# The split of cross head 0's read-back probabilities, moved ahead of head 2's scores

## The chip, the cores and the metric

The kernel runs on one core of a Trainium2 chip. Five engines work from queues of their own: TensorE (PE in the profile; PEld are its weight loads), VectorE (DVE), ScalarE (ACT), GpSimd (POOL) and SyncE (SP), which only issues transfers. The metric is the time of one execution on the device, in microseconds (us). Before the change it is 383.32 us, the median of three runs (382.92 to 384.19).

## What is computed

One decoder layer for 256 tokens of width 1024: a mixer (causal pooling and self-attention in 8 heads), a cross-attention in 4 heads into 256 memory tokens, and a gated feed-forward of width 2816, each followed by a layer norm. The change lies in the cross-attention:

```python
def memory_cross_attention(h, mem, w_xq, w_xkv, w_xo):
    B_, S_, D = h.shape
    M = mem.shape[1]
    q = (h @ w_xq).reshape(B_, S_, XATTN_HEADS, XATTN_HEAD_DIM)
    kv = mem @ w_xkv
    k = kv[..., :D].reshape(B_, M, XATTN_HEADS, XATTN_HEAD_DIM)
    v = kv[..., D:].reshape(B_, M, XATTN_HEADS, XATTN_HEAD_DIM)
    s = jnp.einsum('bshd,bmhd->bhsm', q, k,
                   preferred_element_type=jnp.float32) * (XATTN_HEAD_DIM ** -0.5)
    p = jax.nn.softmax(s, axis=-1)
    o = jnp.einsum('bhsm,bmhd->bshd', p.astype(v.dtype), v).reshape(B_, S_, D)
    return o @ w_xo
```

All of it is float32. The kernel gets there with rounded products: each operand is split into a rounded high half and a low half (what the rounding left), and a product is high x high, high x low and low x high.

## The kernel before

**Splits.** `split` (L318) makes the two halves of a tile: ACT casts it to the high half (L319), DVE subtracts that from the tile to get the low half (L320). The queries are split and scaled in the same way by `split_scaled` (L323 on ACT, L324 on DVE). Weights come in by `Stream`: SP loads a raw tile, ACT casts it (L99), DVE subtracts (L100); tiles are called w0 to w124 in the order of use, with h, l and r for high, low and raw. `three` (L256 to L258) issues the three products of a pair of split operands.

**The cross-attention, head by head** (heads 0 to 3). `do_xq(h)` is a generator of the query projection: 8 steps of 6 products each, for the weights w43 to w50; `run(xq[h], n)` takes n steps. `xscores(h)` makes the scores (12 products into the bank `xs`), the row maximum on DVE (`mx`, L440), the exponentials on ACT (L429), and the scaling on DVE (L434, L436). The probabilities must then be transposed for the product with the values. For heads 0 to 2 this goes through memory: `xprobs_out(h)` turns 32 x 32 blocks on DVE (L340) into a staging tile, also named `xs`, and POOL's queue writes it to memory (`xd<-xs`, L343); `xprobs_in(h)` reads it back in four quarters on the same queue (`xr<-xd`, L351); `xprobs_split(h)` splits what was read back into the pair `xst`. Head 3 is transposed on TensorE instead (`xprobs_pe`, L762). `xattend(h)` multiplies `xst` with the values (12 products into `xo`) and splits the result into `oT`. `project(c_xo, ...)` is the output projection (512-wide products into `acc`), whose steps are run between the heads.

**The staging tiles.** The tiles `xs` (staged), `xr` (read back) and `xst` (split) come from one pool with the tag "pair" and three buffers. A new tile takes a place that is free, and its first writer waits until the last user of that place is done. So where a tile is asked for, in the order of the code, decides whose end it waits for. Before the change the places go round as follows (A, B and C are the three buffers, from the built programs):

| buffer | before | after |
| --- | --- | --- |
| A | xs of head 0, xr of head 1, xst of head 2 | the same |
| B | xr of head 0, xst of head 1, xst of head 3 | xr of head 0, xs of head 2, xr of head 2 |
| C | xs of head 1, xs of head 2, xst of head 0, xr of head 2 | xs of head 1, xst of head 0, xst of head 1, xst of head 3 |

**What sets the order.** The order of each engine's instructions is that of the code (a manual schedule): every call above appends to the engines' queues, and an engine works through its own. The calls around the change are at L775 to L808.

Of the kernel before, what the change touches and what calls it, by code (L numbers as in the profile page):

```python
# [125 lines left out]
def decoder_layer(  # L126
# [183 lines left out]
    def run(gen, n=None):  # L310

        while n is None or n > 0:
            if next(gen, gen) is gen:
                return False
            n = None if n is None else n - 1
        return True

    def split(h, l, ps):  # L318
        nc.scalar.copy(h, ps)  # L319
        nc.vector.tensor_sub(l, ps, r32(h))  # L320
# [408 lines left out]
    def do_xq(h):  # L729
        ps = (bank if h == 0 else accbank)("pxq").rearrange("p (f t) -> p f t", f=2)  # L730
        yield from proj_t([ps[:, f, :] for f in range(2)], c_xq[h], h1T)
        xqT[h] = [sp.tile([P, 2, S], F32R, name=f"xq{i}", tag="pr", bufs=PR_BUFS) for i in range(2)]
        split_scaled(*xqT[h], ps, 256 ** -0.5)

    def xscores(h):
        ps = bank("xs").rearrange("p (t s) -> p t s", t=2)
        for t in range(T):
            for kk in range(2):
                three(ps[:, t, :], pair(xqT[h], ALL, kk, slice(t * P, (t + 1) * P)), pair(xkT, ALL, 2 * h + kk),
                      kk == 0, kk == 1)  # L740
        pr = sp.tile([P, 2, T, P], F32, name="xpr", tag="pr", bufs=PR_BUFS)
        by_t = pr.rearrange("p s t b -> p t s b")
        scaled(by_t, exps(by_t, ps.rearrange("p t (s b) -> p t s b", s=2), negmax(ps)))
        xpr[h] = pr

    def xprobs_out(h):
        turnsx[h] = turned([(0, xpr[h].rearrange("p s t b -> p (s t) b"))], 4, "x", nc.gpsimd)

    def xprobs_in(h):
        turnsx[h] = landed(turnsx[h], 4, "x", queue=nc.gpsimd)  # L750

    def xprobs_split(h):
        raw = turnsx[h].rearrange("p i m b -> p m i b")
        st = sp.tile([P, 2, 2, S], F32R, name="xst", tag="pair", bufs=3)
        xpt[h] = st[:, 0], st[:, 1]
        split(*[x.rearrange("p s (t i b) -> p (s t) i b", t=T, i=4) for x in xpt[h]], raw)
# [18 lines left out]
    xq = [do_xq(h) for h in range(XH)]  # L775
# [10 lines left out]
    run(xq[2])  # L786
    run(xq[3], 3)
    xprobs_in(1)
    run(xq[3], 2)
    xscores(2)  # L790
    xprobs_out(2)
    xprobs_split(0)
    run(xq[3])

    h2 = ap.tile([P, T, D], F32, tag="a8", name="h2")
# [178 lines left out]
```

## Time and profile before

| | us |
| --- | --- |
| median of three runs | 383.32 |
| the profiled execution | 383.19 |
| its span, from its first to its last instruction | 381.4 |
| TensorE busy | 369.1 (97%) |
| VectorE busy | 262.4 (69%) |
| ScalarE busy | 177.6 (47%) |
| GpSimd busy | 34.6 (9%) |

Times inside the profile count from the start of its span. A row of the timeline has the start, the duration, the engine, the line, the operation, what is written `<-` what is read, the shape, and in brackets how long the engine sat idle before it and what ended that. Matmuls overlap, so their pace is read from the distance of their starts, not from their durations. In the list of waits the numbers are the total in us, the count and the longest.

The cross-attention and the start of its output projection lie between about 125 and 180 us. TensorE goes from one product to the next through the whole span, with the exceptions that the prediction shows. In the view of stretches a row has the length, then the busy time of PE, PEld, DVE, ACT and POOL, then TensorE's mean granted clock as a share of full speed, the DMA engines' busy share, and GB/s.

### The profile page before, as it was taken

Reading aid. Unit: us, or ns where it says so; the run is one execution under the profiler, and the core shown is the slowest. Engines: PE = TensorE matmul, PEld = TensorE weight load, DVE = VectorE, ACT = ScalarE, POOL = GpSimd, SP = SyncE. Lnnn points to the kernel's source line nnn. Section 1 sums busy time; section 2 is a strip of 40 time slices with the busy share of each in tenths; the row PEclk is TensorE's granted clock in tenths of the full one; section 3 lists DMA queues with packets and bytes.
Section 4 is the critical chain, followed back from the end, with each engine's and each line's share of the span. In section 5 each row is a group of like instructions: output and inputs, shape, how many; then the busy total and the mean of one; then the engine's idle time right before and its main releaser. Section 6 shows DMA issues by size and latency. Waiting matters only on the chain.

```text
span 381.4 us, 5523 instructions
## 1 busy us (share of the span) xinstructions
PE 369.1 (97%) x2024; PEld 319.0 (84%) x2024; DVE 262.4 (69%) x388; ACT 177.6 (47%) x259; POOL 34.6 (9%) x66
## 2 busy tenths in 40 slices
PE   9999999999999999699999999999999999999992
PEld 9997998997878999588878888888888888888881
DVE  4768898974798976455789866666666666454275
ACT  5756775653153854244229454454545454444000
POOL 1000157140110004120100000000000000000000
PEclk9999999999999999889999999999999999999997
DMA  7997699799337976555106988888789987730011
GB/s 243 411 413 283 232 318 280 257 259 365 115 137 240 384 274 222 159 184 168 56 2 209 380 290 264 232 251 250 236 232 290 296 263 241 211 107 0 0 48 63
DMA packets 32540, 84.52 MB, mean 222 GB/s; under 512 B 4097, under 2 KB 12161, under 8 KB 32385
## 3 DMA queue, kind: packets, MB, share of 16 engines
q1 hardware_dynamic: 30224, 79.05, 63.1%
q0 software_dynamic: 1712, 4.72, 4.0%
q10 hardware_dynamic: 576, 0.39, 0.3%
q8 instruction: 16, 0.26, 0.3%
q14 instruction: 12, 0.09, 0.1%
HBM read 76.81 MB, written 7.34 MB: 221 GB/s over the span
## 4 chain that ended last, share of the span: by engine, by line
PE 81%; issue 11%; DVE 2%; DMA 2%; POOL 2%; ACT 0%; DVEq 0%; POOLq 0%; ACTq 0%
PE pg L258 10%; PE pg L257 10%; PE pg L256 10%; PE acc L256 9%; PE acc L257 9%; PE acc L258 9%; PE pxk L274 6%; PE pqk L392 6%; PE pu L274 3%; DMA xd<-xs 2%; PE busy L363 1%; PE pv L256 1%; POOL xr L351 1%; PE pv L257 1%; PE pv L258 1%
## 5 line engine op out<-in xcount | busy, mean ns | idle before, releaser
L623 POOL TENSOR_TENSOR rs<-rs,mhalf 128x1 f32<-128x1 f32 x6 | 5.4, 898 | 235.4 <-DVE rs L622 235.4
L834 ACT ACTIVATE sg<-pg 128x256 f32<-128x256 f32 x22 | 8.4, 384 | 12.9 <-PE pg L258 12.8
L612 DVE SCALAR_TENSOR_TENSOR r<-h,acc 128x256 f32<-128x256 f32 (+1 forms) x10 | 5.1, 520 | 10.9 <-PE acc L258 10.9
L835 DVE TENSOR_TENSOR sg<-sg,pg 128x256 f32<-128x256 f32 x22 | 9.2, 420 | 4.0 <-ACT sg L834 2.6
L429 ACT ACTIVATE pr<-pr,mx 128x128 f32<-128x128 f32 (+1 forms) x16 | 7.1, 445 | 8.7 <-DVE mx L460 8.7
L351 POOL DMA_DIRECT2D pt<-pd x16 | 8.8, 555 | 7.3 <-DMA pd<-ps 4.5
L320 DVE TENSOR_TENSOR gTl<-gr,gTh 128x512 fp32r<-128x512 f32 x11 | 7.6, 687 | 1.8 <-ACT gTh L319 1.8
L319 ACT CAST gTh<-gr 128x512 fp32r<-128x512 f32 x11 | 6.8, 617 | 4.0 <-DMA gr<-gd 4.0
L319 ACT CAST h2Th<-tp 128x512 fp32r<-128x512 f32 x4 | 2.3, 587 | 13.5 <-PE tp L330 13.4
L615 DVE BATCH_NORM_STATS2 st<-r 128x6 f32<-128x512 f32 (+1 forms) x14 | 8.1, 580 | 0.5
L256 PE MATMUL xo<-xst,xv 128*128 128x256 f32 x16 | 5.2, 326 | 3.3 <-ACT xst L319 3.3
L429 ACT ACTIVATE xpr<-xs,mx 128x256 f32<-128x256 f32 x8 | 3.7, 470 | 9.4 <-DVE mx L440 9.4
L628 DVE SCALAR_TENSOR_TENSOR r<-r,mv,g 128x512 f32<-128x512 f32 x11 | 7.8, 743 | 0.0
L340 DVE STREAM_TRANSPOSE gs<-sg 128x512 f32<-128x512 f32 x11 | 7.7, 704 | 0.0
L351 POOL DMA_DIRECT2D xr<-xd x12 | 6.5, 550 | 12.2 <-PE xo L258 6.8
L343 POOL DMA_DIRECT2D pd<-ps x4 | 2.5, 612 | 51.1 <-DVE ps L340 50.8
L256 PEld LDWEIGHTS xo<-xst,xv 128*128 128x128 f32 x16 | 3.6, 224 | 3.6 <-ACT xst L319 3.5
L320 DVE TENSOR_TENSOR oTl<-xo,oTh 128x512 fp32r<-128x512 f32 x4 | 2.8, 692 | 5.4 <-ACT oTh L319 5.4
L319 ACT CAST oTh<-xo 128x512 fp32r<-128x512 f32 x4 | 2.3, 587 | 7.5 <-PE xo L258 7.5
L434 DVE RECIPROCAL sm<-sm 128x2 f32<-128x2 f32 x12 | 2.0, 165 | 5.5 <-ACT xpr L429 4.4
L436 DVE TENSOR_SCALAR pr<-pr,sm 128x128 f32<-128x128 f32 (+1 forms) x16 | 5.5, 391 | 0.3
L634 DVE SCALAR_TENSOR_TENSOR h<-r,rs,b 128x512 f32<-128x512 f32 x8 | 5.6, 745 | 0.0
(1092 smaller groups left out, 1419.5 us busy)
## 6 DMA issues: line engine op xcount, KB each, us to landing
gd<-gs SPq DMA_DIRECT2D x11, 256.0 KB, 5.1
gr<-gd SPq DMA_DIRECT2D x44, 64.0 KB, 4.7
pd<-ps POOLq DMA_DIRECT2D x4, 384.0 KB, 4.5
pt<-pd POOLq DMA_DIRECT2D x16, 96.0 KB, 7.8
g<-in_ln_g SPq DMA_DIRECT2D x3, 512.0 KB, 7.4
b<-in_ln_b SPq DMA_DIRECT2D x3, 512.0 KB, 7.1
wr<-in_w_qkv SPq DMA_DIRECT2D x5, 256.0 KB, 4.8
mr<-in_mem_t SPq DMA_DIRECT2D x1, 1024.0 KB, 11.2
```

What stands on the lines that cost most here:

```text
L256: nc.tensor.matmul(ps, wa, ya, start=start, stop=False, skip_group_check=part)
L257: nc.tensor.matmul(ps, wa, yb, start=False, stop=False, skip_group_check=part)
L258: nc.tensor.matmul(ps, wb, ya, start=False, stop=stop, skip_group_check=part)
L274: nc.tensor.matmul(pss[f], w[:, s], y, start=k == 0 and f == 0 and n == 0, stop=k == KD - 1 and n == 2, skip_group_check=True)
L319: nc.scalar.copy(h, ps)
L320: nc.vector.tensor_sub(l, ps, r32(h))
L351: queue.dma_start(raw[32 * j:32 * (j + 1)].rearrange("p i m b -> p i (m b)"), via[:, j, :].rearrange("(i a) r -> a i r", i=4))
L392: nc.tensor.matmul(qk[i][:, f, :], w[:, c * P:(c + 1) * P], y, start=k == 0 and f == 0 and w is hi and y is x_hi, stop=k == KD - 1 and w i ...
L429: nc.scalar.activation(dst[:, j, :], src[:, j, :], AF.Exp, bias=mx[:, j:j + 1], scale=sign, accum_out=sm[:, j:j + 1])
L615: nc.vector.bn_stats(self.st[:, self.n, :], self.r[:, c0:c1])
L834: nc.scalar.activation(sg, ps[:, :CW].rearrange("p (f b) -> p f b", f=2), AF.Silu, bias=0.0, scale=1.0)
L835: nc.vector.tensor_mul(sg, sg, ps[:, CW:].rearrange("p (f b) -> p f b", f=2))
```

## The change

`xprobs_split(0)` is called one step of head 3's query projection earlier than head 2's scores, instead of behind `xprobs_out(2)`. Nothing is added, removed or resized.

```diff
     run(xq[3], 3)
     xprobs_in(1)
-    run(xq[3], 2)
+    run(xq[3], 1)
+    xprobs_split(0)
+    run(xq[3], 1)
     xscores(2)
     xprobs_out(2)
-    xprobs_split(0)
     run(xq[3])
```

On ACT the place is behind the cast of w56, where the exponentials of head 2 stood (both names are without buffer numbers; DMASW and a digit is the counter of a transfer on POOL's queue, and the level that is awaited is not shown):

```order
 L99 CAST w56h<-w56r 128x1024 [waits DMAHW7_49]
-L429 ACTIVATE xpr,sm<-xs,mx 128x2x128 [waits DVE_49]
-L429 ACTIVATE xpr,sm<-xs,mx 128x2x128
 L319 CAST xst<-xr 128x512 [waits DMASW5_49,DMASW6_49,DMASW1_49,DMASW7_49,DMASW0_49,DVE_49]
+L429 ACTIVATE xpr,sm<-xs,mx 128x2x128 [waits DVE_49]
+L429 ACTIVATE xpr,sm<-xs,mx 128x2x128
 L99 CAST w57h<-w57r 128x1024 [waits DMAHW0_49,PE_49]
 L323 ACTIVATE xq_1869<-pxq 128x512 [waits PE_49,Activation_49]
```

The cast of head 0's `xst` now stands ahead of head 2's two exponentials. The counters 5, 6, 7 and 0 are those of the four quarters of head 0's read-back, 1 is that of head 1's write-out, and 6 is used again for head 2's write-out: before the change the level awaited on it is one transfer higher.

On DVE the place is behind the subtraction for w56; what follows up to the new queries of head 3 (`xq_1870`) is head 2's softmax and the turning of its blocks:

```order
 L100 TENSOR_TENSOR w56l<-w56r,w56h 128x1024 [waits DMAHW7_49,Activation_49]
+L320 TENSOR_TENSOR xst<-xr,xst 128x512 [waits DMASW5_49,DMASW6_49,DMASW1_49,DMASW7_49,DMASW0_49,Activation_49]
 L440 TENSOR_REDUCE mx<-xs 128x2 [waits PE_49]
 L434 RECIPROCAL sm<-sm 128x2 [waits Activation_49]
 L436 TENSOR_SCALAR xpr<-xpr,sm 128x2x128 [waits DVE_49]
 L436 TENSOR_SCALAR xpr<-xpr,sm 128x2x128
-L340 STREAM_TRANSPOSE xs<-xpr 128x4x4x32 [waits DMASW1_49,DVE_49]
-L320 TENSOR_TENSOR xst<-xr,xst 128x512 [waits DMASW6_49,DMASW5_49,DMASW7_49,DMASW0_49,Activation_49]
+L340 STREAM_TRANSPOSE xs<-xpr 128x4x4x32 [waits DMASW3_49,DVE_49]
 L100 TENSOR_TENSOR w57l<-w57r,w57h 128x1024 [waits DMAHW0_49,PE_49,Activation_49]
 L324 SCALAR_TENSOR_TENSOR xq_1870<-pxq,xq_1869 128x512 [waits Activation_49]
```

The subtraction moved ahead of head 2's maximum, and head 1's write-out (counter 1) is now awaited by the split and no longer by the turning of head 2's blocks, which waits on 3 for a much earlier write-out of the self-attention that used buffer B.

On POOL, behind head 2's write-out, the order of transfers is the same; the read-back of head 2 begins with another wait, since it goes to another buffer:

```order
 L343 DMA xd<-xs 128x512 [waits DMASW6_49,DVE_49]
-L351 DMA xr<-xd 32x4x128 [waits DMAHW1_49,DMAHW2_49,DMASW7_49,DMAHW3_49,DMASW6_49,DMAHW4_49,DVE_49,PE_49]
-L351 DMA xr<-xd 32x4x128 [waits DMASW0_49]
-L351 DMA xr<-xd 32x4x128
+L351 DMA xr<-xd 32x4x128 [waits DMASW6_49,DMASW7_49,DMASW0_49,Activation_49]
+L351 DMA xr<-xd 32x4x128 x2
 L351 DMA xr<-xd 32x4x128 [waits DMASW2_49]
```

It waited for TensorE before (the attention of head 0, whose `xst` held buffer C) and now for the write-out of head 2 and for ACT. On TensorE and SP no instruction moves.

## Prediction

> **What bounds the kernel now.** I read the page's busy times first, then the list of who waited for whom, then the chain that ended last, and only then the matmuls one by one.
>
> ```profile
> PE 369.1 (97%) x2024; PEld 319.0 (84%) x2024; DVE 262.4 (69%) x388; ACT 177.6 (47%) x259; POOL 34.6 (9%) x66
> ...
> PE xo L256 <- ACT xst L319: 3.3, 1, 3.3
> PE busy L363 <- PEq L938: 0.8, 1, 0.8
> PE tp L330 <- DVE h L634: 0.3, 1, 0.3
> PE xv L256 <- DVE r L612: 0.3, 1, 0.3
> ```
>
> The first row says that TensorE (PE) sets the time: 97% of a span of 381.4 us. The others are all the waits of its matmuls. One is large: 3.3 us at the first product of the attention of cross head 0 (`xo`), for ScalarE's half of the split `xst`. The chain of waits says what this cast itself waited for:
>
> ```profile
> 147.82 2.56 DMA xd<-xs
> ...
> 155.02 2.77 DMA xd<-xs
> ...
> 157.97 0.63 ACT xst L319
> 158.62 0.70 DVE xst L320
> ...
> 159.37 0.58 PE xo L257
> ```
>
> The cast started 0.18 us after the write-out `xd<-xs` issued at 155.02 had landed (155.02 + 2.77 = 157.79). That is head 2's write-out, which has nothing to do with head 0's data. It matters because `xst` was put in the place of head 2's staging tile `xs`. Head 0's own data had been read back long before; the rows for the four quarters of head 0, then of head 1, are:
>
> ```profile
> 144.07 2.18 POOL L351 DMA_DIRECT2D xr<-xd  x4 [2.85 <-DMA xd<-xs]
> DMA to landing us min/median/max: 3.6/3.8/4.3
> ...
> 150.91 2.17 POOL L351 DMA_DIRECT2D xr<-xd  x4 [2.53 <-DMA xd<-xs]
> DMA to landing us min/median/max: 4.2/5.0/5.5
> ```
>
> The last quarter of head 0 was issued about 145.7 (144.07 + 3 x 0.55), so it had landed by 145.7 + 4.3 = 150.0 at the latest. The matmuls around the hole, each row's first column being its start:
>
> ```profile
> 149.74 0.28 PE L256 MATMUL xs<-xkTh,xq 128*128 128x256 f32 x1
> ...
> 151.18 0.28 PE L274 MATMUL pxq<-h1Th,w49h 128*128 128x256 f32 x1
> ...
> 155.02 0.28 PE L274 MATMUL pxq<-h1Th,w50l 128*128 128x256 f32 x1
> 158.64 0.58 PE L256 MATMUL xo<-xst,xv 128*128 128x256 f32 x1 [3.34 <-ACT xst L319]
> 159.37 0.58 PE L257 MATMUL xo<-xst,xv 128*128 128x256 f32 x1
> ...
> 161.88 0.41 PE L256 MATMUL xs<-xkTh,xq 128*128 128x256 f32 x1
> ...
> 164.44 0.63 PE L256 MATMUL acc<-w51h,oTh 128*128 128x512 f32 x1
> ...
> 165.55 0.40 PE L256 MATMUL acc<-w51h,oTh 128*128 128x512 f32 x1
> ...
> 167.63 0.28 PE L256 MATMUL xo<-xst,xv 128*128 128x256 f32 x1
> ```
>
> Undisturbed, the 12 products of head 2's scores take 151.18 - 149.74 = 1.44 us, 0.12 us a start; nine 512-wide products take 167.63 - 165.55 = 2.08 us, 0.231 a start. Behind the hole the same 12 scores (161.88 to 164.44) take 2.56 us. The stretches, with the granted clock (third number from the right), say why:
>
> ```profile
> 158.00:159.00 1.00, 0.36 (x1) 0.29 (x1) 0.38 (x1) 1.00 (x2) 0.00 (x0) 0.75 0.00 0
> 160.00:165.00 5.00, 5.00 (x24) 4.90 (x24) 3.00 (x5) 1.13 (x3) 2.17 (x4) 0.50 0.64 211
> 165.00:166.00 1.00, 1.00 (x5) 0.79 (x4) 0.37 (x1) 0.59 (x3) 0.00 (x0) 0.83 0.83 217
> 106.00:108.00 2.00, 1.72 (x9) 1.11 (x7) 1.93 (x4) 1.52 (x2) 0.00 (x0) 1.00 0.60 244
> ```
>
> The clock fell to 0.50 at about 158.5 (0.75 is half a microsecond of it) and came back at about 165.34 (0.83 is a third), so it was low for 6.8 us; after the 0.28 us rest near 107.9 it stayed at 1.00. The hole costs twice: the wait, and the slow matmuls behind it. [...]
>
> **The change part by part.** Nothing is added or removed: one cast on ACT and one subtraction on DVE stand earlier, ahead of head 2's exponentials and maximum. TensorE's own order is the same.
>
> *What goes.* From the last query product (155.02) to head 1's attention (167.63) TensorE takes 12.61 us before. Undisturbed, it is 25 starts of 0.12 (itself, 12 `xo`, 12 `xs`) and 12 of 0.231: 3.00 + 2.77 = 5.77. The surplus is **6.84 us**, made of the wait 158.64 - 155.14 = 3.50; the second product's wait for the subtraction, 0.73 - 0.12 = 0.61; 23 slow starts, (164.44 - 159.37) - 23 x 0.12 = 2.31; and 12 partly slow wide ones, 3.19 - 2.77 = 0.42.
>
> *What is late next.* The split now takes the place of head 1's staging tile, free when head 1's write-out lands at 147.82 + 2.56 = 150.38, later than its data (150.0). I take the reaction of 0.18 us seen above. ACT and DVE then stand thus in the trace of before:
>
> ```profile
> 148.69 1.04 ACT L99 CAST w56h<-w56r 128x1024 fp32r<-128x1024 f32 x1
> 152.11 0.47 ACT L429 ACTIVATE xpr<-xs,mx 128x256 f32<-128x256 f32 x1 [2.37 <-DVE mx L440]
> ...
> 158.50 1.04 ACT L99 CAST w57h<-w57r 128x1024 fp32r<-128x1024 f32 x1
> 159.44 0.59 ACT L323 ACTIVATE xq<-pxq 128x512 fp32r<-128x512 f32 x1
> ...
> 172.96 0.62 ACT L319 CAST xst<-xr 128x512 fp32r<-128x512 f32 x1
> ...
> 146.81 0.71 DVE L340 STREAM_TRANSPOSE xs<-xpr 128x512 f32<-128x512 f32 x1
> 147.45 1.19 DVE L100 TENSOR_TENSOR w55l<-w55r,w55h 128x1024 fp32r<-128x1024 f32 x1
> ...
> 151.38 0.69 DVE L440 TENSOR_REDUCE mx<-xs 128x2 f32<-128x512 f32 x1 [0.39 <-PE xs L258]
> 153.16 0.17 DVE L434 RECIPROCAL sm<-sm 128x2 f32<-128x2 f32 x1 [1.09 <-ACT xpr L429]
> ...
> 154.01 0.71 DVE L340 STREAM_TRANSPOSE xs<-xpr 128x512 f32<-128x512 f32 x1
> ...
> 159.57 1.23 DVE L100 TENSOR_TENSOR w57l<-w57r,w57h 128x1024 fp32r<-128x1024 f32 x1 [0.26 <-ACT w57h L99]
> 160.71 0.68 DVE L324 SCALAR_TENSOR_TENSOR xq<-pxq,xq 128x512 fp32r<-128x512 f32 x1
> ...
> 162.38 2.17 POOL L351 DMA_DIRECT2D xr<-xd  x4 [6.80 <-PE xo L258]
> ```
>
> ACT is free from 148.69 + 1.04 = 149.73 to 152.11, so the cast runs 150.56 to 151.18: hidden. DVE subtracts from 151.20 to 151.89, idle before, and its next instruction follows 0.64 later, as 147.45 follows 146.81: head 2's maximum starts at 151.84 where it was 151.38, so head 2's chain is 0.46 us late. The tiles that TensorE needs at 155.14 are whole at 151.9: **no wait there**, with 3.2 us to spare, and no cause for the clock to fall.
>
> Behind the maximum on DVE stand head 2's scaling, its transpose (154.01 - 151.38 = 2.63 later), the split of w57 (0.64 later) and, 160.71 - 159.57 = 1.14 after that, the low half of head 3's queries (L324): 151.84 + 2.63 + 0.64 + 1.14 = 156.25, done at 156.93. ACT does not hold it up. Its exponentials are read by DVE 153.16 - 152.11 = 1.05 after their start, now at 153.6, so the cast of w57, stuck until 158.50 before, ends by 153.6 + 1.04 = 154.6, ahead of DVE's turn at 155.1. The high half of the queries follows the last query product, 155.02 + 0.28 + 0.59 = 155.9. TensorE now reaches head 3's scores at 155.14 + 1.44 = 156.58 and wants the low half at its third product, 156.82. From DVE's end to a start I take 0.15 us: between 158.62 + 0.70 = 159.32 and 159.37 lay 0.05 where only the streamed operand was awaited, and the low half is a weight, whose load comes first. It starts at 157.08, and **0.25 us** comes back as a new wait. Its bounds are 0 (if the DVE chain closes up by some tenths) and 1.1 (if head 0's last quarter takes 5.5 us, the longest in the rows above, and so lands at 151.2 instead of 150.38). I take 0.25, since every term but that landing is a row.
>
> *Other moves.* POOL's read-back of head 2 stood until 162.38 behind head 0's attention; now it waits for its own write-out (155.02 + 0.46 + 2.77 = 158.25) and issues its four DMAs from about 158.7, 3.7 us earlier. The last is issued at about 160.4 and lands by 160.4 + 5.5 = 165.9; ACT wants it at 172.96 - 6.6 = 166.4. If it is later, TensorE still has the time until it comes to that head. Head 1's read-back has landed by 150.91 + 3 x 0.55 + 5.5 = 158.1; its split, due on ACT at about 157.3 behind head 0's attention, may wait 0.8 us, while TensorE wants it at 161.0. So both are costed at nothing. Later splits are released by TensorE and move with it; SP's weight loads, released by those splits, come earlier too, and no matmul waits for a load in the list above.
>
> The sum: 6.84 - 0.25 = 6.6 us off the profiled execution's span, 381.4 to 374.8; around the span lay 383.19 - 381.4 = 1.8 us, so **376.6 us**. That execution is 0.13 us below the median of the runs, 383.32.
>
> **The rivals.**
>
> *A late quarter on the other side.* ACT and DVE take their work in order, so the moved split can hold head 2's softmax, w57 and head 3's queries. From a landing L it is 0.18 to the cast, 156.93 - 150.56 = 6.37 to the end of L324 and 0.15 to the product, so head 3's third score starts at L + 6.70; before it was at 162.3 (two slow starts behind 161.88). So the change loses from L = 155.6 on, a quarter 9.9 us on its way where the longest took 5.5. At L = 157.8, as late as the wait of now, it costs 157.8 + 6.70 - 162.3 = 2.2 us: 385.4. [...] Chance 0.02.
>
> *A larger remainder.* The new wait at L324 is a whole microsecond, because the write-out of head 1 or a quarter lands later: 376.6 + (1.1 - 0.25) = 377.4. For: landings spread from 3.6 to 5.5. Chance 0.09.
>
> *The clock falls all the same.* Were a rest of a few tenths at L324 enough, the 2.31 + 0.42 = 2.7 us of slow matmuls would stay: 379.3. Against: the 0.28 us rest at 107.9 kept 1.00. Chance 0.05.
>
> *It doesn't do what it says, or gives all back.* If the split still had to wait for a write-out, or a later transfer became the bound, the time is 383.2. Against: the change's rows name head 1's write-out, and no other wait of TensorE is over 0.8 us. Chance 0.03.
>
> **How the numbers follow.** My forecast has 0.81. The range takes the forecast with its bounds (376.35 without the remainder) and the larger remainder, 0.90 together, widened by what runs differ (382.92 to 384.19 before): 375.8 to 378.3. A measurement of this kernel tells 0.3%, 1.15 us, from no change; faster than that are the forecast, the larger remainder and the fallen clock: 0.95; within it, 0.03; slower, 0.02.
>
> **What would show it.** In the changed profile the 3.3 us wait of `xo` should be gone from TensorE's list; the cast of `xst` should start near 150.6, head 2's maximum near 151.8; TensorE should start `xo` near 155.1 and head 1's attention near 161.0; the clock should be 1.00 from 150 to 170; a wait of some 0.2 us should stand before the third product of head 3's scores. I am wrong if the clock dips there with no long rest, or if the 6.6 us gained by 168 are smaller at the end.

## The result

The changed kernel takes 377.12 us (median of six runs, 376.74 to 377.74) where the kernel before took 383.12 us beside it (six runs, 381.51 to 385.4). The ratio is 0.984, with a 95% interval of 0.9806 to 0.9874. In a later session it was 376.61 us against 382.53 us, ratio 0.985 (0.9829 to 0.9871). So the change gains 6.0 and 5.9 us by the medians; 6.6 was forecast. The profiled execution took 376.74 us with a span of 374.9 us; 374.8 was forecast.

The page's first row after the change, and then all the waits of TensorE's matmuls:

```profile
PE 365.9 (98%) x2024; PEld 316.6 (84%) x2024; DVE 262.3 (70%) x388; ACT 177.8 (47%) x259; POOL 34.6 (9%) x66
...
PE busy L363 <- PEq L939: 0.8, 1, 0.8
PE tp L330 <- DVE h L634: 0.4, 1, 0.4
PE xv L256 <- DVE r L612: 0.3, 1, 0.3
PE po L496 <- DMA pt<-pd: 0.2, 1, 0.2
```

The row `PE xo L256 <- ACT xst L319: 3.3` is gone, and nothing of its size has come in. Around the place where the hole was, the timeline of TensorE (start, duration) reads:

```profile
155.22 0.28 PE L274 MATMUL pxq<-h1Th,w50l 128*128 128x256 f32 x1
155.34 0.28 PE L256 MATMUL xo<-xst,xv 128*128 128x256 f32 x1
155.46 0.28 PE L257 MATMUL xo<-xst,xv 128*128 128x256 f32 x1
...
156.78 0.28 PE L256 MATMUL xs<-xkTh,xq 128*128 128x256 f32 x1
...
157.05 0.39 PE L258 MATMUL xs<-xkTh,xq 128*128 128x256 f32 x1
...
158.34 0.40 PE L256 MATMUL acc<-w51h,oTh 128*128 128x512 f32 x1
...
161.09 0.28 PE L256 MATMUL xo<-xst,xv 128*128 128x256 f32 x1
```

`xo` follows the last query product after 0.12 us, as any other product does, and the scores of head 3 run at 0.12 a start instead of 0.21. The granted clock (third number from the right) stays whole:

```profile
154.00:158.00 4.00, 4.00 (x35) 3.93 (x34) 3.36 (x6) 2.06 (x4) 0.56 (x1) 1.00 0.89 295
158.00:159.00 1.00, 1.00 (x8) 0.91 (x7) 0.89 (x2) 0.37 (x1) 0.31 (x1) 1.00 1.03 348
160.00:165.00 5.00, 5.00 (x29) 4.39 (x28) 3.40 (x6) 3.23 (x7) 0.87 (x2) 1.00 0.52 148
```

On ACT, DVE and POOL the moved split and what stands behind it:

```profile
150.69 0.62 ACT L319 CAST xst<-xr 128x512 fp32r<-128x512 f32 x1 [0.75 <-DMA xd<-xs]
152.67 0.47 ACT L429 ACTIVATE xpr<-xs,mx 128x256 f32<-128x256 f32 x1 [1.36 <-DVE mx L440]
...
153.58 1.04 ACT L99 CAST w57h<-w57r 128x1024 fp32r<-128x1024 f32 x1
...
151.34 0.69 DVE L320 TENSOR_TENSOR xst<-xr,xst 128x512 fp32r<-128x512 f32 x1
151.95 0.68 DVE L440 TENSOR_REDUCE mx<-xs 128x2 f32<-128x512 f32 x1
...
156.31 0.68 DVE L324 SCALAR_TENSOR_TENSOR xq<-pxq,xq 128x512 fp32r<-128x512 f32 x1
...
158.69 2.18 POOL L351 DMA_DIRECT2D xr<-xd  x4 [2.55 <-ACT xst L319]
```

The cast still waits for a write-out, but for head 1's, and that wait lies in time that ACT had free. The low half of head 3's queries (L324) is ready at 156.99, and its product starts at 157.05.

A measure that serves below is the way from the last query product to head 1's attention, less the 5.77 us of undisturbed starts in it. It was 12.61 - 5.77 = 6.84 us before; it is 161.09 - 155.22 - 5.77 = 0.10 us now. I call it the surplus.

### The profile page after: what moved, and what is told of

The parts are those of the page before. It is cut to its first block, busy times and chain, and to the rows that moved or that the text cites. A ratio compares the mean times of both kernels' runs of the same rounds, so it can differ in the third digit from the quotient of the medians.

```text
span 374.9 us, 5523 instructions
## 1 busy us (share of the span) xinstructions
PE 365.9 (98%) x2024; PEld 316.6 (84%) x2024; DVE 262.3 (70%) x388; ACT 177.8 (47%) x259; POOL 34.6 (9%) x66
## 4 chain that ended last, share of the span: by engine, by line
PE 90%; DVE 4%; DMA 2%; ACT 1%; issue 1%; POOL 0%; DVEq 0%; ACTq 0%
PE pg L257 10%; PE pg L256 10%; PE pg L258 10%; PE acc L256 9%; PE acc L258 9%; PE acc L257 9%; PE pqk L392 6%; PE pxq L274 6%; PE pxk L274 5%; DMA pt<-pd 2%; PE xv L256 2%; PE xv L258 2%; PE xv L257 2%; PE pu L274 2%; PE busy L363 1%; PE pv L256 1%
## 5 line engine op out<-in xcount | busy, mean ns | idle before, releaser
L319 ACT CAST h2Th<-tp 128x512 fp32r<-128x512 f32 x4 | 2.4, 588 | 13.5 <-PE tp L330 13.4
L319 ACT CAST gTh<-gr 128x512 fp32r<-128x512 f32 x11 | 6.8, 617 | 3.4 <-DMA gr<-gd 3.4
L363 PE MATMUL busy<-const-float32-0.0 128*128 128x128 f32 x18 | 4.2, 428 | 0.8 <-PEq L939 0.8
L508 POOL TENSOR_TENSOR win<-win 128x269 f32<-128x269 f32 (+2 forms) x6 | 4.9, 815 | 0.5
L343 POOL DMA_DIRECT2D xd<-xs x3 | 1.7, 576 | 34.6 <-DVE xs L340 34.6
```

## The experiments

The theory: head 0's split waited because of its place in the pool, the wait let the clock fall, and both go with the place. Rivals: the earlier position on ACT and DVE is what pays; the matmuls behind the hole are slow for another reason; and, for the side that loses, the moved split holds what stands behind it on ACT and DVE.

### Another place, the order of before

```diff
-        st = sp.tile([P, 2, 2, S], F32R, name="xst", tag="pair", bufs=3)
+        if h == 0:
+            st = nmp.tile([P, 2, 2, S], F32R, name="xst", tag="r", bufs=2)
+        else:
+            st = sp.tile([P, 2, 2, S], F32R, name="xst", tag="pair", bufs=3)
```

> The kernel before with one difference: head 0's split xst lies in a buffer of its own (one of the two of the norm's row tiles, idle here), so it waits for no staging tile; every engine's order is that of before. Theory (the place in the pool is what costs): the cast starts right behind head 2's exponentials, near 153.0 instead of 157.97, the subtraction behind the turning of head 2's blocks, near 154.7; TensorE starts xo near 155.1, the clock stays at 1.00, and with some 0.35 us of small waits the time is about 376.7 us (the hole of 6.84 us less 0.35). Rival (the earlier position on ACT and DVE is what pays): 383 us, as before.

376.82 us against 382.33 us, ratio 0.9863 (0.9846 to 0.988). The split on ACT and DVE and the first products of `xo` in its profile:

```profile
152.72 0.61 ACT L319 CAST xst<-xr 128x512 fp32r<-128x512 f32 x1
...
154.34 0.65 DVE L320 TENSOR_TENSOR xst<-xr,xst 128x512 fp32r<-128x512 f32 x1
...
154.84 0.28 PE L256 MATMUL xo<-xst,xv 128*128 128x256 f32 x1
155.05 0.39 PE L257 MATMUL xo<-xst,xv 128*128 128x256 f32 x1
```

The cast has no wait at all, in its old position behind the exponentials. The second product is late by 0.1 us for the subtraction, and the surplus is 160.82 - 154.72 - 5.77 = 0.33 us, where 0.35 was expected. The place alone pays the whole gain; that the split also stands earlier adds nothing that these runs can tell.

### The split between the scores and the staging of head 2

```diff
     xscores(2)
-    xprobs_out(2)
     xprobs_split(0)
+    xprobs_out(2)
```

> The split of head 0 stands between head 2's scores and its staging: ACT's order is that of before, on DVE only the subtraction and the turning of head 2's blocks change places; the places in the pool are those of the change. Theory (place): 376.6 to 377.0 us, cast near 153.0, no fall of the clock, head 2's maximum not late. Rival (the position ahead of the exponentials matters): clearly slower than the change, 380 us or more.

376.62 us against 382.33 us, ratio 0.9869 (0.9844 to 0.9894). Here the code asks for the split's tile just ahead of head 2's staging tile, and of head 2's work only the turning of its blocks is held up; the surplus is 160.87 - 154.76 - 5.77 = 0.34 us. It was run once more beside the changed kernel:

> The split between head 2's scores and its staging, once more beside the changed kernel. Theory (only the place counts): equal to the changed kernel within 0.4 us. Rival (it is the better version, since head 2's softmax isn't held up): lower by more than that.

> The changed kernel once more, on the chip and in the rounds of the next three. Theory (the clock stretch of before is 3.4 us in most executions, so the hole is worth about 5.4 us and the new wait 0.1): 376.5 to 377.0 us where the kernel before has 382.0 to 382.6, a gain of 5.2 to 5.7 us; clock 1.00 from 150 to 170. Rival (the first profile's 6.84 us is the typical hole): a gain of 6.6 us.

376.66 us (0.9859, 0.984 to 0.9877) and 376.61 us (0.985, 0.9829 to 0.9871): equal. In this second profile of the changed kernel the product that waits for L324 came 0.28 us late (157.17 where 156.89 was due), so the surplus was 161.21 - 155.09 - 5.77 = 0.35 us. The remainder of 0.25 in the forecast lies between the two profiles. No version here beats the changed kernel.

### The hole kept, but filled

```diff
     xprobs_split(0)
     run(xq[3])
+    keep_busy(14)
```

> The kernel before, with 14 products of constants that write a bank nobody reads, put ahead of head 0's attention on TensorE, in the hole of 3.3 us (14 x 0.23 = 3.2 us). The output is the same. Theory (the hole costs twice, 4.11 us of waits and 2.73 us of slow matmuls): the wait for the cast remains until 158.6, but the clock stays at 1.00 and the 2.7 us come back: 380.5 us. Rival (the matmuls behind the hole are slow for another reason, as the weight loads or the tiles of the split): 383 us, clock 0.50 as before.

381.09 us against 382.33 us, ratio 0.9972 (0.9961 to 0.9983). The wait is there, the fall of the clock is not:

```profile
158.78 0.38 PE L256 MATMUL xo<-xst,xv 128*128 128x256 f32 x1 [0.15 <-ACT xst L319]
...
155.00:158.00 3.00, 3.00 (x29) 3.00 (x28) 0.00 (x0) 0.00 (x0) 0.56 (x1) 1.00 0.61 214
158.00:159.00 1.00, 0.85 (x7) 0.62 (x5) 0.24 (x1) 0.89 (x2) 0.00 (x0) 1.00 0.00 0
160.00:165.00 5.00, 4.74 (x32) 4.16 (x31) 3.65 (x6) 2.47 (x8) 2.18 (x4) 1.00 0.62 204
```

So idleness of TensorE is what makes the matmuls behind the hole slow, and the two costs can be had apart. But only 1.2 us came back where 2.7 were expected. Some of the gap is a new wait of about 0.4 us at head 3's third score: at full speed TensorE gets there before L324 is done. The surplus of this profile is 165.63 - 155.22 - 5.77 = 4.64 us, which is 2.2 below the 6.84 of the first profile of the kernel before. For the medians to differ by only 1.2, the kernel before must often have a smaller surplus than in that profile. So it was profiled again.

### The kernel before, profiled twice more

> The kernel before, profiled once more. [...] Rival (the fall follows the hole alone): 6.8 us again and the same time, 382 to 383 us.

> The kernel before, profiled a third time; the expectations are those of before_a.

One execution each: 381.55 us (span 379.8) and 382.57 us (span 380.8). In the first of them:

```profile
154.88 0.28 PE L274 MATMUL pxq<-h1Th,w50l 128*128 128x256 f32 x1
158.27 0.38 PE L256 MATMUL xo<-xst,xv 128*128 128x256 f32 x1 [3.11 <-ACT xst L319]
158.99 0.58 PE L257 MATMUL xo<-xst,xv 128*128 128x256 f32 x1 [0.34 <-DVE xst L320]
...
166.00 0.28 PE L256 MATMUL xo<-xst,xv 128*128 128x256 f32 x1
...
158.00:159.00 1.00, 0.39 (x2) 0.20 (x2) 0.69 (x1) 1.00 (x2) 0.00 (x0) 0.89 0.00 0
160.00:162.00 2.00, 2.00 (x12) 2.00 (x11) 1.02 (x2) 0.26 (x1) 0.00 (x0) 0.50 0.26 92
162.00:163.00 1.00, 1.00 (x9) 1.00 (x9) 0.64 (x2) 0.85 (x2) 1.00 (x2) 0.91 1.01 377
```

and in the second:

```profile
159.00:160.00 1.00, 0.53 (x2) 0.34 (x3) 0.69 (x1) 1.00 (x3) 0.00 (x0) 0.99 0.00 0
160.00:162.00 2.00, 2.00 (x10) 2.00 (x11) 1.82 (x2) 0.51 (x2) 0.00 (x0) 0.50 0.00 0
162.00:163.00 1.00, 1.00 (x7) 1.00 (x6) 0.00 (x0) 0.49 (x2) 0.23 (x1) 0.50 0.73 258
163.00:164.00 1.00, 1.00 (x9) 1.00 (x9) 0.87 (x2) 0.62 (x2) 1.00 (x3) 0.80 0.98 385
```

The clock is low from 158.78 (0.89 leaves 0.22 of that microsecond at 0.50) to 162.18, and from 159.98 to 163.40: 3.4 us both times, half of the 6.8 us of the first profile, with the same hole. The surplus is 166.00 - 154.88 - 5.77 = 5.35 us in the first of these, made of (158.27 - 155.00) + (0.72 - 0.12) = 3.87 of waits and 1.48 of slow starts; in the second it is 5.59, of which 4.02 and 1.57. So the waits repeat within 0.25 us, and the slow starts cost 1.5, 1.6 or 2.7 us. The length of the low stretch differs from execution to execution; 6.8 us came in neither of these two.

### The read-back delayed

This is the changed kernel with head 0's read-back issued later, to see the losing side of the moved split.

```diff
-    run(xq[2], 3)
-    xprobs_in(0)
-    run(xq[2], 2)
+    run(xq[2], 5)
     xscores(1)
     xprobs_out(1)
+    xprobs_in(0)
```

> The changed kernel, with head 0's read-back issued behind head 1's write-out on POOL's queue instead of ahead of it, so that it is issued from about 150.9 and lands near 157.3 (quarters took 4.2 to 5.5 us then). Theory (ACT and DVE work in order, the moved split holds head 2's softmax, w57 and head 3's queries): xo starts near 158.1 and the third product of head 3's scores near L + 6.7 = 164.0, 1.7 us later than before the change, with a second rest of some 4 us ahead of it and a low clock behind that: 385 to 387 us. Rival (only the split's own lateness counts): xo near 158.1 and no second rest, 380 to 383 us.

381.6 us against 382.33 us, ratio 0.9964 (0.9938 to 0.999), but its ten runs lie in groups: three from 378.66 to 379.12, one at 380.23, six from 381.59 to 382.64. The landing was misjudged in the expectation. Head 0's read-back doesn't wait for head 1's write-out, only for its turn on POOL's queue, so it was issued from 148.16. The profile (378.86 us):

```profile
152.93 0.62 ACT L319 CAST xst<-xr 128x512 fp32r<-128x512 f32 x1 [3.58 <-DMA xr<-xd]
...
157.41 0.39 PE L256 MATMUL xs<-xkTh,xq 128*128 128x256 f32 x1 [1.06 <-ACT xq L323]
...
159.28 0.39 PE L258 MATMUL xs<-xkTh,xq 128*128 128x256 f32 x1 [1.37 <-DVE xq L324]
```

From the cast to the third score it is 159.28 - 152.93 = 6.35 us; the prediction's chain gives 6.37 + 0.15 = 6.52. The wait isn't at `xo`, which started on time at 154.75, but behind it at head 3's scores, on both halves of its queries: the moved split holds its followers, as the first rival of the prediction says. The clock stayed at 1.00. Three more profiles looked for the upper group:

> The kernel of l1_late, profiled once more; its ten runs fell into two groups, about 378.9 and about 381.8 us, and the profile caught one of the first, with a clock of 1.00 throughout. Theory (the rests of 1.1 and 1.4 us ahead of head 3's scores suffice for a fall of the clock in some executions): a run of the second group shows a stretch at 0.50 behind 159 us that costs about 2.9 us, with the same order and the same waits. Rival (the late read-back itself varies): the clock stays at 1.00 and the waits are about 2.9 us longer.

> The kernel of l1_late, profiled a third time; the expectations are those of l1_a.

> The kernel of l1_late, profiled a fourth time; the expectations are those of l1_a.

The first two were 378.55 and 378.97 us, with the same two waits (1.1 and 1.4 us) and a clock of 1.00. The last was 381.54 us (eight runs, 381.18 to 381.92, against 382.53; ratio 0.9982, 0.9967 to 0.9998):

```profile
153.91 0.62 ACT L319 CAST xst<-xr 128x512 fp32r<-128x512 f32 x1 [4.67 <-DMA xr<-xd]
...
158.40 0.38 PE L256 MATMUL xs<-xkTh,xq 128*128 128x256 f32 x1 [1.52 <-ACT xq L323]
160.27 0.39 PE L258 MATMUL xs<-xkTh,xq 128*128 128x256 f32 x1 [1.37 <-DVE xq L324]
...
161.00:162.00 1.00, 1.00 (x8) 1.00 (x7) 0.41 (x1) 0.00 (x0) 0.13 (x1) 0.63 0.96 377
162.00:164.00 2.00, 2.00 (x6) 1.52 (x6) 0.86 (x2) 1.25 (x5) 2.00 (x4) 0.50 0.98 348
164.00:165.00 1.00, 1.00 (x5) 0.80 (x4) 0.88 (x3) 0.71 (x1) 0.04 (x1) 0.66 0.53 152
```

Theory and rival both have a part. The landing came 1.0 us later, and the third score with it (again 6.36 us behind the cast). On top, two rests of 1.5 and 1.4 us, with two products between them, let the clock fall from about 161.3 to 164.7. From the third score to head 1's attention (165.90) it took 5.63 us, where the first profile took 163.32 - 159.28 = 4.04: 1.6 us for the slow starts. The mean clock of each run of `l1_late` divides its ten runs alike: 0.994 or 0.995 in the four up to 380.23 us, 0.987 to 0.990 in the other six.

### The hole half filled

```diff
     xprobs_split(0)
     run(xq[3])
+    keep_busy(7)
```

> As b14_busy with 7 products of constants, which fill the first half of the hole and leave a rest of about 1.7 us. [...]

381.98 us against 382.53 us, ratio 0.9981 (0.9965 to 0.9997), in two groups: four runs from 380.73 to 380.94, six from 381.96 to 382.62. The profile is one of the lower group (380.91 us): a rest of 1.8 us, and no fall.

```profile
PE xo L256 <- ACT xst L319: 1.8, 1, 1.8
...
160.00:165.00 5.00, 4.74 (x30) 4.12 (x29) 3.62 (x7) 2.59 (x7) 2.18 (x4) 1.00 0.58 221
```

The medians of the two groups lie 1.3 us apart, close to the 1.5 us of a fall of 3.4 us. No run of the upper group was profiled. The mean clock of each run points to a fall in five of its six: 0.992 or 0.993, where the lower group has 0.996 or 0.997, and 3.4 us at half clock take 1.7 of 381 us, 0.0045. The sixth, of 382.06 us, has 0.997, so it was longer for another reason, which stays open. The mean also counts the low clock at the program's end (0.50 from 376.96 to 381.4 in the first profile of before), so this is support and no proof.

## Why the prediction was right

It forecast 376.6 us within 375.8 to 378.3; 377.12 and 376.61 were measured.

**The wait.** Right. The second product apart, 3.50 us of TensorE's wait hung on head 2's write-out through the split's place. With another place and the same order it is gone; with the place of the change it is gone too, wherever the split stands.

**What is late next.** Right in kind and size: no wait at `xo`; the moved split hidden on ACT at 150.69 (150.56 forecast); head 2's maximum at 151.95 (151.84); L324 done at 156.99 (156.93). The new wait was forecast at 0.25 us and is 0.1 in one profile and 0.35 in the other. DVE's end to the product took 0.06 us and not 0.15: the rows of its weight load and of the product itself both start at 157.05.

**The clock.** Right in kind: it stays whole, and filling the hole shows that it was the hole which made it fall. Wrong in size for the median run: the term 2.31 + 0.42 = 2.7 us was read from one execution, the only one shown, whose clock stayed low for 6.8 us. Two others had 3.4 us and 1.5 and 1.6 us of slow starts. One execution had decided a term that differs between executions. With these two the hole is worth 5.4 to 5.6 us, less 0.1 to 0.35; with the first one 6.5 to 6.7. The medians' 5.9 to 6.0 lie between. The mean clocks of the runs say that neither length is rare: of the 38 runs of the kernel before in the two rounds of experiments, 17 have a mean clock of 0.984 or 0.985, as the first profile (0.985), with a median of 382.57 us; 15 have 0.992 or 0.993, as the two others (0.992), with a median of 381.73 us; six lie between. The profiled pair gives 6.5 because the first profile of before, at 383.19 us, was one with the long stretch; its other runs go down to 381.22 us. The absolute forecast, 376.6 us, did not suffer: the 383.19 us it starts from hold the same long stretch that the sum takes off.

**Other moves.** Right. Head 1's cast waited 0.18 us for its read-back; head 2's read-back, issued from 158.69 to 160.3, was wanted at 166.43; the gain stood to the end: 6.84 - 0.10 less the 0.20 us by which this execution was later at 155 is 6.5, the difference of the spans.

**The rivals.** The late quarter is real: the delayed read-back puts head 3's scores where the chain says. Its break-even, though, was worked out from waits alone (L = 155.6). With a landing at 153.7 the kernel took 381.54 us already, less than 1 us below the kernel before, since its rests brought the clock down as well. The rival that a rest of some tenths lets the clock fall didn't occur: behind the 0.34 and 0.27 us in the profile of the filled hole it stayed at 1.00, and behind the product that came 0.28 us late in the changed kernel; rests of 1.4 and 1.5 us did it in one profile and not in three with 1.1 and 1.4.

## What to carry to other kernels

A tile's place in a shared pool can tie it to a transfer that has nothing to do with its data: where a cast waits for a write-out of something else, ask which tile lay there, and ask for the tile before the newer one takes the free place. A hole in TensorE's work can cost its length and then a stretch of slow matmuls (here 3.9 to 4.1 us of waits and 1.5 to 2.7 us of slow starts); both should be summed, the second one from several executions, since its length isn't the same in each (3.4 and 6.8 us at 0.50 here). When a step is moved ahead on an engine that works in order, price what stands behind it by the chain to the next wait of TensorE, here to 0.2 us, and ask whether that wait lets the clock fall.

## What the runs showed of the hardware

The clock's fall did not begin with the rest. It came at 158.51, 3.2 us into the rest and just before work resumed at 158.64, but also 0.5 us (158.78 after 158.27), 0.9 us (159.98 after 159.12) and 1.0 us (161.26 after 160.27) behind the resumption, in the same program or nearly so. The low stretch was 3.4 us in three profiles and 6.8 us in one. The rests of TensorE that the timelines show there, those below 1 us left out:

| profile | rests, us | granted clock behind them | low for, us |
| --- | --- | --- | --- |
| before, first | 3.34 | 0.50 | 6.83 |
| before, second | 3.11 | 0.50 | 3.40 |
| before, third | 3.25 | 0.50 | 3.42 |
| read-back delayed, last | 1.52 and 1.37 | 0.50 | 3.42 |
| hole half filled | 1.77 | 1.00 | |
| read-back delayed, first | 1.06 and 1.37 | 1.00 | |
| read-back delayed, second | 1.09 and 1.37 | 1.00 | |
| read-back delayed, third | 1.11 and 1.36 | 1.00 | |

The longest rest alone doesn't sort them: 1.77 us had no fall behind it in one profile, and rests of 1.52 and 1.37 us, with two products between them, had one. What sets the moment of the fall, and why the clock was low for 6.8 us in one profile and for 3.4 us in three, these runs do not show.

Fourteen products of constants in the hole, which took 3.29 us, kept the clock at 1.00 in the profile. They held nothing up: `xo` started 3.56 us behind the last query product, where it was 3.39 to 3.62 us without them. They gave back 1.2 us, the smaller part of what the hole costs.
